# FFN down projection: from seven block products on all 22 contraction tiles to seven on 12 and plain products on 10, with the sums on VectorE

## The chip, the cores and the metric

One core of a Trainium2 chip runs the kernel. The metric is device time in microseconds (us) of one execution; less is better. Besides TensorE (PE in the profile, its weight loads PEld), the core has VectorE (DVE), ScalarE (ACT), GpSimd (POOL) and SyncE (SP), which here issues loads. Each engine works through its own queue in order and waits at semaphores.

## The reference

An encoder block on 512 tokens of width 1024, all in float32: three parallel mixers, a gated merge, an output projection, then the feed-forward network, which the change is about:

```python
def conv_glu_ffn(h, w_up, w_conv, b_conv, w_down):
    a, u = jnp.split(h @ w_up, 2, axis=-1)
    return (jax.nn.gelu(dwconv3(a, w_conv, b_conv)) * u) @ w_down
...
    x = x + conv_glu_ffn(rms_norm(x, ffn_norm_g[l]), w_ffn_up[l], w_ffn_conv[l], b_ffn_conv[l], w_ffn_down[l])
return rms_norm(x, final_norm_g)
```

`h` is 512 x 1024, `w_up` 1024 x 5632, `w_down` 2816 x 1024.

## The kernel before

**Float32 products in three matmuls.** Every operand is split into a high part (ScalarE copies it, rounded, to float32r) and a low part (VectorE subtracts the high part from the source). `mm3` (L192) then issues high x high, high x low, low x high: three matmuls (L193, L194, L195), each 128 x 128 stationary with 512 moving columns.

**Up projection** (loop `for f in range(FT)`, L1331; 22 tiles of 128 hidden columns). For each `f` there are two weight blocks, `ua` and `uu`, of 8 contraction tiles, so 48 matmuls. Each block of 128 x 1024 is loaded (L151) three blocks ahead, and split in two halves (L175 high on ScalarE, L176 low on VectorE) one block ahead, into a ring of four high and four low buffers (`wh`, `wl`). The columns of `ua` then go through a convolution in three steps (L437 to L441) and a gelu (L1355 to L1358); GpSimd multiplies by the norm (L1359), VectorE by the columns of `uu` (L1367). For the first tiles `turn` also transposes the residual on TensorE.

**Down projection.** The 22 contraction tiles are taken as a 2 x 2 block matrix product: rows (two halves of the tokens, `HS` = 256), contraction (two halves of `HF` = 11 tiles), columns (two halves of `S` = 512). Seven block products p1, p5, p6, p3, p7, p2, p4 of sums of blocks replace eight. Each runs over 11 contraction tiles with two token tiles, so 6 matmuls for each weight tile and 462 in all. The sums of weight blocks are made during the up stage: `sum_load` (L1252) loads one contraction tile of all four blocks (1 MB), GpSimd forms four sums (L1261, L1262, L1263, L1258) and stores them to `tdn` in DRAM (L1259). The sums of activations are made by `ops_to` (L1297): the sum on GpSimd (L1309, L1317, L1319), high part on ScalarE (L1322), low part on VectorE (L1324), and p5's further step on VectorE (L1326).

**What sets the order around the change.** A loop over the 77 (product, tile) pairs (L1429) asks for loads four steps ahead (`raws_to`, 1 MB each for four tiles into a unit buffer), for sums two or three steps ahead, and for split tiles four ahead (`tiles_to`, into the same rings of four). Every fourth tile's low part in four of the products is GpSimd's:

```python
A.activation(h, src, AF.Copy)
eng = G if k % 4 == 3 and PRODUCTS[p][0] in ("p1", "p7", "p2", "p4") else V
eng.tensor_tensor(l, src, h.bitcast(F32), op=ALU.subtract)
```

`add` (L1384) adds a finished product to the residual in `xt`: VectorE from PSUM, and for p6 and p7 GpSimd from SBUF (L1395). `unit()` gives one of 15 buffers of 128 x 2112 float32 (`u` in the rows); a load into a unit waits until the last reader of its former content is done. In p4 the last four tiles are done token tile by token tile, the last of them in two column halves, so that the final norm (`squares` L1399, `power` on GpSimd, scale, store) of the earlier rows runs beside them. The framework orders the instructions of each engine when the program is built, so a queue's order isn't the order of the code.

Of the kernel before, what the change touches and what calls it, by code (L numbers as in the profile page):

```python
# [11 lines left out]
F32 = mybir.dt.float32  # L12
# [5 lines left out]
P = 128  # L18
S = 512
# [6 lines left out]
HF = FT // 2  # L26
# [35 lines left out]
def block_list():  # L62
# [19 lines left out]
    for hh in range(2):  # L82
        for f in range(HF * hh, HF * (hh + 1)):
            L.append((("ua", f), 1024))
            L.append((("uu", f), 1024))
# [17 lines left out]
def hybrid_block(ctx, tc, xg, xT, memT, wflat, wdn, vecs, gbias, nabias, out):  # L103
# [1142 lines left out]
    GROUPS = ((0, 4), (4, 8), (8, HF))  # L1246
    B11, B12, B22, B21 = range(4)
    tdn = dp.tile([4, P, HF * S], F32, name="tdn")
# [3 lines left out]
    def sum_load(k):  # L1252
        w = unit()[:, :4 * S]
        SY.dma_start(w.rearrange("p (q n) -> p q n", q=4), wdn[:, :, k * S:(k + 1) * S].rearrange("q p n -> p q n"))
        q = [w[:, i * S:(i + 1) * S] for i in range(4)]

        def store():
            G.tensor_tensor(q[B21], q[B21], q[B22], op=ALU.subtract)  # L1258
            G.dma_start(tdn[:, :, k * S:(k + 1) * S].rearrange("q p n -> p q n"), w.rearrange("p (q n) -> p q n", q=4))  # L1259

        sums.extend([lambda: G.tensor_tensor(q[B11], q[B12], q[B11], op=ALU.subtract),  # L1261
                     lambda: G.tensor_tensor(q[B12], q[B22], q[B12], op=ALU.subtract),  # L1262
                     lambda: G.tensor_tensor(q[B22], q[B22], q[B11], op=ALU.subtract),  # L1263
                     store])


    PRODUCTS = (("p1", wdn, B11), ("p5", tdn, T1), ("p6", tdn, T2), ("p3", wdn, B22), ("p7", tdn, T3), ("p2", wdn, B21),
                ("p4", tdn, T4))
    STEPS = [(p, g) for p in range(7) for g in range(3)]
    TILES = [(p, k) for p in range(7) for k in range(HF)]  # L1270
    uu_ = [[None] * 3 for _ in range(2)]
# [3 lines left out]
    def raws_to(n):  # L1275
        while ahead["raw"] < min(n, len(STEPS)):
            p, g = STEPS[ahead["raw"]]
            a, b = GROUPS[g]
            w = unit()[:, :(b - a) * S]
            SY.dma_start(w, PRODUCTS[p][1][PRODUCTS[p][2], :, a * S:b * S])  # L1280
            for k in range(a, b):
                wraw[p, k] = w[:, (k - a) * S:(k - a + 1) * S]
            ahead["raw"] += 1

    def tiles_to(n):
        while ahead["tile"] < min(n, len(TILES)):
            p, k = TILES[ahead["tile"]]
            src = wraw.pop((p, k))
            h = wp.tile([P, HWT], F32R, tag="hi", name=nm("wh"), bufs=4)[:, :S]
            l = wp.tile([P, HWT], F32R, tag="lo", name=nm("wl"), bufs=4)[:, :S]  # L1290
            A.activation(h, src, AF.Copy)  # L1291
            eng = G if k % 4 == 3 and PRODUCTS[p][0] in ("p1", "p7", "p2", "p4") else V
            eng.tensor_tensor(l, src, h.bitcast(F32), op=ALU.subtract)  # L1293
            wsp[p, k] = h, l
            ahead["tile"] += 1

    def ops_to(n):  # L1297
        while ahead["op"] < min(n, len(STEPS)):
            p, g = STEPS[ahead["op"]]
            name = PRODUCTS[p][0]  # L1300
            nk = GROUPS[g][1] - GROUPS[g][0]
            v = [uu_[i][g][:, :nk * S].rearrange("p (k s) -> p k s", k=nk) for i in range(2)]
            a11, a21, a12, a22 = v[0][:, :, :HS], v[0][:, :, HS:], v[1][:, :, :HS], v[1][:, :, HS:]
            u = unit(F32R)
            h, l = u[:, :nk * HS], u[:, 4 * HS:(4 + nk) * HS]
            r3 = lambda t: t.rearrange("p (k s) -> p k s", s=HS)
            srcs = [(0, nk, {"p1": a11, "p6": a11, "p7": a21, "p2": a12, "p4": a22}.get(name))]
            if name == "p6":
                G.tensor_tensor(a11, a22, a21, op=ALU.subtract)  # L1309
            elif srcs[0][2] is None:  # L1310
                srcs = []
                for k in range(0, nk, 2):
                    m = min(2, nk - k)
# [13 lines left out]
            ops[p, g] = h, l  # L1327
            ahead["op"] += 1

    UR = []  # L1330
    for f in range(FT):  # L1331
        i, j = divmod(f, HF)
        if j % 4 == 0:
            uu_[i][j // 4] = unit()
        UR.append(uu_[i][j // 4][:, j % 4 * S:(j % 4 + 1) * S])
# [23 lines left out]
        G.tensor_tensor(c, c, rb2, op=ALU.mult)  # L1359
        for _ in range(3):  # L1360
            if sums:
                sums.pop(0)()
# [7 lines left out]
        if 2 <= f < FT and f * 3 // 4 - 1 < HF and (f * 3 // 4) != ((f - 1) * 3 // 4):  # L1370
            sum_load(f * 3 // 4 - 1)
# [5 lines left out]
    gfin = wp.tile([P, BW], F32, tag="raw", name=nm("wr"), bufs=3)[:, :D]  # L1377
# [6 lines left out]
    def add(name):  # L1384
        for t in range(2):
# [6 lines left out]
            for c in {"p1": ((0, 0),), "p5": ((0, 1), (1, 1)), "p3": ((0, 1),), "p2": ((0, 0),)}.get(name, ()):  # L1392
# [9 lines left out]
    def power(n):  # L1402
        v, col = tiny(1), tiny(1)
        V.tensor_scalar(v, n[0], n[1], EPS, op0=ALU.add, op1=ALU.add)
        for s in n[2:]:
            V.tensor_tensor(v, v, s, op=ALU.add)
# [3 lines left out]
    def finish(t):  # L1410
        n = []
        squares(t, n, 0, S)
        squares(t, n, S, D)
        col = power(n)
        V.scalar_tensor_tensor(xt[t], xt[t], col, gfin, op0=ALU.mult, op1=ALU.mult)
        SY.dma_start(out[t * P:(t + 1) * P, :], xt[t])

    part = {2: [], 3: []}
    TAIL = HF - 4

    def mms(p, k, t, cs=slice(0, S), ps=None, first=0, end=HF - 1):
        name = PRODUCTS[p][0]
        g, kk = divmod(k, 4)
        h, l = ops[p, g]
        wh, wl = wsp[p, k]
        q = slice(kk * HS + t * P, kk * HS + (t + 1) * P)
        mm3(banks[name][t] if ps is None else ps, h[:, q], l[:, q], wh[:, cs], wl[:, cs], k == first, k == end)

    for j, (p, k) in enumerate(TILES):  # L1429
        name = PRODUCTS[p][0]  # L1430
        last = name == "p4"
        if k == 0:
            pool = atps if name in ("p1", "p5", "p7", "p2") else mmps
            banks[name] = [pool(), pool()]
        if k % 4 == 0:
            i = STEPS.index((p, k // 4))
            raws_to(i + 4)
            ops_to(i + 2 if i == 0 else i + 3)
        tiles_to(j + 4)
        if k == 3 and p > 0:  # L1440
            add(PRODUCTS[p - 1][0])
        if k == 7 and name == "p2":
            for t in (2, 3):
                squares(t, part[t], S, D)
                V.tensor_tensor(xt[t][:, S:], xt[t][:, S:], gfin[:, S:], op=ALU.mult)  # L1445
        if k == 7 and last:
            for t in range(2):
                finish(t)
        if last and k >= TAIL:
            if k == HF - 1:  # L1450
# [134 lines left out]
```

## Time and profile before

| | us |
|---|---|
| timed runs, median of 3 | 884.86 (882.9 to 886.56) |
| the profiled execution's own time | 883.9 |
| its span on the core | 882.0 |
| mean granted TensorE clock | 0.996 |

The page gives for each engine its busy time, share of the span and number of instructions. A row of the timeline gives start, duration, engine, line, operation, output<-inputs, shapes, and in brackets the idle time before it with what ended that. A row of the waits reads: engine, tile and line <- who was waited for: total us, times, longest. In the rows `wr` and `u` are loaded weights, `wh` and `wl` their parts, `mm` and `at` PSUM banks, `s` scratch.

### The profile page before, as it was taken

Reading aid. Unit: us, or ns where it says so; the run is one execution under the profiler, and the core shown is the slowest. Engines: PE = TensorE matmul, PEld = TensorE weight load, DVE = VectorE, ACT = ScalarE, POOL = GpSimd, SP = SyncE. Lnnn points to the kernel's source line nnn. Section 1 sums busy time; section 2 is a strip of 40 time slices with the busy share of each in tenths; the row PEclk is TensorE's granted clock in tenths of the full one; section 3 lists DMA queues with packets and bytes.
Section 4 is the critical chain, followed back from the end, with each engine's and each line's share of the span. In section 5 each row is a group of like instructions: output and inputs, shape, how many; then the busy total and the mean of one; then the engine's idle time right before and its main releaser. Section 6 shows DMA issues by size and latency. Waiting matters only on the chain. (4 is left out here: it accounts for less than half of the span.)

```text
span 882.0 us, 12121 instructions
## 1 busy us (share of the span) xinstructions
PE 858.5 (97%) x4146; PEld 718.5 (81%) x4146; DVE 674.0 (76%) x1306; ACT 486.6 (55%) x1015; POOL 241.6 (27%) x283
## 2 busy tenths in 40 slices
PE   9999999999999999999999999999899999789986
PEld 7898889888888888888888888888787888568865
DVE  7794789996476768897585668778887876989775
ACT  7563476864455668897444453434343444355744
POOL 0101100000435262400000005555665414631142
PEclk9999999999999999999999999999999999999999
DMA  8324633533434363533233425666685533444712
GB/s 271 100 78 153 199 123 101 179 103 96 119 98 105 87 169 120 146 123 111 98 96 122 145 91 205 226 236 234 217 289 177 189 127 133 178 147 153 263 78 96
DMA packets 46014, 131.92 MB, mean 150 GB/s; under 512 B 6008, under 2 KB 11128, under 8 KB 44160
## 3 DMA queue, kind: packets, MB, share of 16 engines
q1 hardware_dynamic: 35168, 112.90, 38.5%
q0 software_dynamic: 10352, 17.85, 6.7%
q8 instruction: 33, 0.54, 0.3%
q10 hardware_dynamic: 432, 0.39, 0.1%
q14 instruction: 29, 0.24, 0.1%
HBM read 115.38 MB, written 15.75 MB: 149 GB/s over the span
## 5 line engine op out<-in xcount | busy, mean ns | idle before, releaser
L195 PE MATMUL mm<-u,wl 128*128 128x512 f32 (+1 forms) x907 | 350.5, 387 | 2.9 <-DVE wl L176 2.9
L193 PE MATMUL mm<-u,wh 128*128 128x512 f32 (+1 forms) x907 | 353.2, 390 | 0.0
L194 PE MATMUL mm<-u,wh 128*128 128x512 f32 (+1 forms) x907 | 349.7, 386 | 0.0
L175 ACT ACTIVATE wh<-wr 128x512 fp32r<-128x512 f32 (+1 forms) x256 | 157.9, 625 | 149.9 <-PE mm L194 117.3
L176 DVE TENSOR_TENSOR wl<-wr,wh 128x512 fp32r<-128x512 f32 (+2 forms) x258 | 196.7, 765 | 47.4 <-ACT wh L175 46.2
L195 PEld LDWEIGHTS mm<-u,wl 128*128 128x128 f32 x907 | 170.3, 188 | 38.9 <-DVE wl L176 4.5
L194 PEld LDWEIGHTS mm<-u,wh 128*128 128x128 f32 x907 | 170.6, 188 | 32.9
L193 PEld LDWEIGHTS mm<-u,wh 128*128 128x128 f32 x907 | 170.6, 188 | 32.6
L1359 POOL TENSOR_TENSOR s<-s,rb 128x512 f32<-128x512 f32 x22 | 36.3, 1648 | 250.3 <-PE mm L195 163.5
L519 POOL DMA_DIRECT2D u<-nav_d x128 | 62.3, 520 | 70.1 <-DVE X L200 25.1
L1293 DVE TENSOR_TENSOR wl<-u,wh 128x512 fp32r<-128x512 f32 x69 | 58.6, 881 | 7.5 <-ACT wh L1291 7.3
L194 PE MATMUL at<-wl,u 128*128 128x512 f32 (+2 forms) x152 | 54.5, 359 | 10.1 <-DVE wl L1293 5.7
L1291 ACT ACTIVATE wh<-u 128x512 fp32r<-128x512 f32 x77 | 46.8, 625 | 30.5 <-PE at L195 12.9
L193 PE MATMUL at<-wh,u 128*128 128x512 f32 (+2 forms) x152 | 53.2, 350 | 2.5 <-ACT wh L1291 2.5
L439 ACT ACTIVATE s<-pad,vec 128x512 f32<-128x512 f32 x30 | 24.4, 813 | 52.9 <-DVE pad L437 52.9
L195 PE MATMUL at<-wh,u 128*128 128x512 f32 (+2 forms) x152 | 52.9, 348 | 0.0
L194 PE MATMUL mm<-wl,u 128*128 128x512 f32 (+1 forms) x118 | 45.2, 383 | 0.4 <-DVE wl L1293 0.4
L195 PE MATMUL mm<-wh,u 128*128 128x512 f32 (+1 forms) x118 | 45.1, 382 | 0.0
L193 PE MATMUL mm<-wh,u 128*128 128x512 f32 (+1 forms) x118 | 44.9, 382 | 0.0
L194 PEld LDWEIGHTS at<-wl,u 128*128 128x128 f32 x152 | 28.9, 190 | 18.2 <-DVE wl L1293 10.4
L1367 DVE SCALAR_TENSOR_TENSOR u<-mm,s 128x512 f32<-128x512 f32 x22 | 15.2, 691 | 26.7 <-POOL s L1359 26.7
L193 PEld LDWEIGHTS at<-wh,u 128*128 128x128 f32 x152 | 28.8, 190 | 7.0 <-ACT wh L1291 3.3
(338 smaller groups left out, 1233.5 us busy)
## 6 DMA issues: line engine op xcount, KB each, us to landing
wr<-wflat SPq DMA_DIRECT2D x125, 512.0 KB, 3.4
u<-wdn SPq DMA_DIRECT2D x17, 1024.0 KB, 6.7
tdn<-u POOLq DMA_DIRECT2D x11, 1024.0 KB, 5.0
u<-tdn SPq DMA_DIRECT2D x8, 1024.0 KB, 5.3
nab<-nabias SPq DMA_DIRECT2D x16, 256.0 KB, 2.7
u<-nav_d POOLq DMA_DIRECT2D x128, 32.0 KB, 2.8
s<-xT SPq DMA_DIRECT2D x15, 256.0 KB, 3.8
u<-tdn SPq DMA_DIRECT2D x4, 768.0 KB, 4.4
```

The source lines that it names most:

```text
L175: A.activation(h[:, u:v], src, AF.Copy)
L176: V.tensor_tensor(l[:, u:v], src, h[:, u:v].bitcast(F32), op=ALU.subtract)
L193: PE.matmul(ps, lh, rh, start=start, stop=False)
L194: PE.matmul(ps, lh, rl, start=False, stop=False)
L195: st["mm"] = PE.matmul(ps, ll, rh, start=False, stop=stop).ins
L439: A.activation(t1, pad[:, 0:512], AF.Identity, scale=vcol(w, i), bias=vcol(b, i))
L519: G.dma_start(vw[r * 32:(r + 1) * 32, i * 256:(i + 1) * 256], nav_v[hf, r, CW[b]:CW[b] + 32, hp * 256:(hp + 1) * 256])
L1291: A.activation(h, src, AF.Copy)
L1293: eng.tensor_tensor(l, src, h.bitcast(F32), op=ALU.subtract)
L1359: G.tensor_tensor(c, c, rb2, op=ALU.mult)
L1367: V.scalar_tensor_tensor(UR[f], pu, 0.5, c, op0=ALU.mult, op1=ALU.mult)
```

## The change

1. The block product now covers only the first 12 contraction tiles (`WN` = 6 in each half). The other 10 (`SN`) are multiplied plainly: column half 1 as segment c1, all 10 tiles behind p3; column half 0 as segments c0, one or two tiles at a time between the products, and its last four at the end. Products and plain segments add up in the same PSUM banks where they can (c1 on p3's; p2 and p4 on c0's).
2. All elementwise sums of this part move from GpSimd to VectorE: the norm factor in the up loop, the sums of weight blocks (now 6 loads for 11), those of activations, the low parts and the adds of products. GpSimd keeps the six stores to `tdn` and the powers of the norm.
3. For f of 12 and more the up loop writes the high and low part of its result itself (`split_act`), since these tiles are used as they are.
4. Weights of the down stage come two tiles (512 KB) at a time for four (1 MB), into the `raw` ring of three buffers for every second load and into a unit otherwise.
5. In the final norm of the last row the second half's sum carries the first half's along (a column of 257), so the sum of the two needs no instruction behind it.

```diff
-HF = FT // 2
+WN = 6
+SN = FT - 2 * WN
+SEGMENTS = (("p1", None), ("c0", (0,)), ("p5", None), ("c0", (1,)), ("p6", None), ("c0", (2,)), ("p3", None),
+            ("c1", range(SN)), ("c0", (3, 4)), ("p7", None), ("p2", None), ("c0", (5,)), ("p4", None),
+            ("c0", range(6, SN)))
...
         def store():
-            G.tensor_tensor(q[B21], q[B21], q[B22], op=ALU.subtract)
+            V.tensor_tensor(q[B21], q[B21], q[B22], op=ALU.subtract)
...
-        sums.extend([lambda: G.tensor_tensor(q[B11], q[B12], q[B11], op=ALU.subtract),
+        sums.extend([lambda: V.tensor_tensor(q[B11], q[B12], q[B11], op=ALU.subtract),
...
     def raws_to(n):
-        while ahead["raw"] < min(n, len(STEPS)):
-            p, g = STEPS[ahead["raw"]]
-            a, b = GROUPS[g]
-            w = unit()[:, :(b - a) * S]
+        while ahead["raw"] < min(n, len(LOADS)):
+            i = ahead["raw"]
+            name, ks, _ = LOADS[i]
+            w = wp.tile([P, BW], F32, tag="raw", name=nm("wr"), bufs=3) if i < 3 or i % 2 else unit()
+            w = w[:, :len(ks) * S]
+            src, q = PRODUCTS[name] if name in PRODUCTS else (wst, int(name[1]))
+            SY.dma_start(w, src[q, :, ks[0] * S:(ks[-1] + 1) * S])
...
             A.activation(h, src, AF.Copy)
-            eng = G if k % 4 == 3 and PRODUCTS[p][0] in ("p1", "p7", "p2", "p4") else V
-            eng.tensor_tensor(l, src, h.bitcast(F32), op=ALU.subtract)
+            V.tensor_tensor(l, src, h.bitcast(F32), op=ALU.subtract)
...
             if name == "p6":
-                G.tensor_tensor(a11, a22, a21, op=ALU.subtract)
+                V.tensor_tensor(a11, a22, a21, op=ALU.subtract)
...
-                        G.tensor_tensor(t, a21[:, sl], a22[:, sl], op=ALU.add)
+                        V.tensor_tensor(t, a21[:, sl], a22[:, sl], op=ALU.add)
                     else:
-                        G.tensor_tensor(t, a12[:, sl], a11[:, sl], op=ALU.subtract)
+                        V.tensor_tensor(t, a12[:, sl], a11[:, sl], op=ALU.subtract)
...
-        G.tensor_tensor(c, c, rb2, op=ALU.mult)
-        for _ in range(3):
-            if sums:
-                sums.pop(0)()
+        V.tensor_tensor(c, c, rb2, op=ALU.mult)
...
-        V.scalar_tensor_tensor(UR[f], pu, 0.5, c, op0=ALU.mult, op1=ALU.mult)
+        if f < 2 * WN:
+            V.scalar_tensor_tensor(ur, pu, 0.5, c, op0=ALU.mult, op1=ALU.mult)
+        else:
+            V.tensor_tensor(c, pu, c, op=ALU.mult)
...
+            split_act(UH[-1], UL[-1], c, 0.5)
...
             for c in {"p6": ((0, 1),), "p7": ((1, 1), (1, 0))}.get(name, ()):
-                G.tensor_tensor(cell(c, t), cell(c, t), Q[t], op=ALU.add)
+                V.tensor_tensor(cell(c, t), cell(c, t), Q[t], op=ALU.add)
...
+    def plain(name, k, t, ps, cs, start, stop):
+        wh, wl = wsp[name, k]
+        tsl = slice(t * P, (t + 1) * P)
+        mm3(ps, UH[k][:, tsl], UL[k][:, tsl], wh[:, cs], wl[:, cs], start, stop)
```

Three places of the engines' queues. Line numbers of the changed kernel are a little higher: L176 is L179 there, L1293 is L1303, L1359 is L1370, L1324 is L1332, L1280 is L1292; a number behind a name is that of the buffer's use.

**VectorE in the up stage, at tile f = 4.** Before, from the convolution's first step (`pad`) to the product with `uu` (L1367):

```order
L437 TENSOR_TENSOR pad0_137<-mm_1120_5922,rb_2_5625 128x512
L176 TENSOR_TENSOR wl_1127_5969<-wr_1106_5867,wh_1126_5968 128x512
L440 SCALAR_TENSOR_TENSOR s_1121_5948<-pad0_137,vec_78,s_1121_5948 128x512
L441 SCALAR_TENSOR_TENSOR s_1121_5948<-pad0_137,vec_78,s_1121_5948 128x512
L176 TENSOR_TENSOR wl_1133_6009<-wr_1115_5912,wh_1132_6008 128x512
L1356 SCALAR_TENSOR_TENSOR s_1122_5952<-s_1122_5952,s_1121_5948 128x512
L1358 SCALAR_TENSOR_TENSOR s_1121_5948<-s_1122_5952,s_1121_5948 128x512
L176 TENSOR_TENSOR wl_1135_6013<-wr_1115_5912,wh_1134_6012 128x512
L1367 SCALAR_TENSOR_TENSOR u_1114_5911<-mm_1128_5972,s_1121_5948 128x512
```

Now, from its second step (L443) on:

```order
L443 SCALAR_TENSOR_TENSOR s_1121_5945<-pad0_137,vec_78,s_1121_5945 128x512
L1264 TENSOR_TENSOR u_1114_5907<-u_1114_5907 128x512
L444 SCALAR_TENSOR_TENSOR s_1121_5945<-pad0_137,vec_78,s_1121_5945 128x512
L179 TENSOR_TENSOR wl_1133_6005<-wr_1115_5909,wh_1132_6004 128x512
L1265 TENSOR_TENSOR u_1114_5907<-u_1114_5907 128x512
L1367 SCALAR_TENSOR_TENSOR s_1122_5949<-s_1122_5949,s_1121_5945 128x512
L1266 TENSOR_TENSOR u_1114_5907<-u_1114_5907 128x512
L179 TENSOR_TENSOR wl_1135_6009<-wr_1115_5909,wh_1134_6008 128x512
L1369 SCALAR_TENSOR_TENSOR s_1121_5945<-s_1122_5949,s_1121_5945 128x512
L1261 TENSOR_TENSOR u_1114_5907<-u_1114_5907 128x512
L1370 TENSOR_TENSOR s_1121_5945<-s_1121_5945,rb_2_5625 128x512
```

The four sums of the weight blocks in `u_1114` and the norm factor (L1370) have moved in between the steps of the gelu and the low parts of the next blocks.

**From the up to the down stage.** Before, GpSimd's queue at the end of the up stage: sums of p5 (L1317) and p6 (L1309), the norm factor of the last up tile (L1359), and the low parts of p1's fourth and eighth tile (L1293):

```order
L1309 TENSOR_TENSOR u_1048_5547<-u_1225_6560,u_1048_5547 128x4x256
L1359 TENSOR_TENSOR s_1379_7455<-s_1379_7455,rb_2_5625 128x512
L1293 TENSOR_TENSOR wl_1395_7515<-u_1372_7417,wh_1394_7514 128x512
L1317 TENSOR_TENSOR s_1430_7658<-u_1178_6285,u_1344_7254 128x256
L1309 TENSOR_TENSOR u_1114_5911<-u_1285_6910,u_1114_5911 128x4x256
L1293 TENSOR_TENSOR wl_1408_7570<-u_1373_7419,wh_1407_7569 128x512
```

Now VectorE's queue at the same place, from the norm factor on (`mm_1383` is the last `uu`):

```order
L1370 TENSOR_TENSOR s_1377_7441<-s_1377_7441,rb_2_5625 128x512
L1303 TENSOR_TENSOR wl_1395_7505<-wr_1371_7405,wh_1394_7504 128x512
L1378 TENSOR_TENSOR s_1377_7441<-mm_1383_7459,s_1377_7441 128x512
L1303 TENSOR_TENSOR wl_1399_7517<-wr_1389_7493,wh_1398_7516 128x512
L1303 TENSOR_TENSOR wl_1402_7529<-wr_1389_7493,wh_1401_7528 128x512
L203 SCALAR_TENSOR_TENSOR u_1356_7320<-s_1377_7441,u_1356_7320 128x512
L1332 TENSOR_TENSOR u_1403_7538<-s_1404_7539,u_1403_7538 128x512
L1332 TENSOR_TENSOR u_1403_7538<-s_1405_7541,u_1403_7538 128x256
L1334 TENSOR_TENSOR u_1048_5547<-u_1048_5547 128x3x256
L1325 TENSOR_TENSOR s_1407_7549<-u_1098_5818,u_1195_6376 128x512
L1325 TENSOR_TENSOR s_1408_7551<-u_1098_5818,u_1195_6376 128x256
L1303 TENSOR_TENSOR wl_1410_7559<-wr_1390_7495,wh_1409_7558 128x512
```

The low parts of p1's tiles 4 to 6 and of c0's first tile (`wl_1410`) share one queue with the sums and low parts of p5's activations; GpSimd has nothing there.

**The weight loads of p5 and p6 in SyncE's queue.** Before, four tiles (three at a product's end) in each:

```order
L1280 DMA u_1390_7505<-tdn_5546 128x2048 [waits DMASW5_49,DMASW2_49,PE_49]
L1280 DMA u_1402_7554<-tdn_5546 128x2048 [waits DMASW7_49,DMASW1_49,PE_49]
L1280 DMA u_1415_7609<-tdn_5546 128x1536 [waits DMAHW4_49,DMASW2_49,DMAHW7_49,DVE_49,Pool_49]
L1280 DMA u_1427_7653<-tdn_5546 128x2048 [waits DMAHW5_49,PE_49]
L1280 DMA u_1441_7711<-tdn_5546 128x2048 [waits DMAHW6_49,DMAHW2_49,DVE_49]
```

Now, with two tiles of p5 (`u_1400`, `wr_1411`, `u_1416`) or p6 (`u_1427`, `wr_1435`, `u_1440`) or p3 (`wr_1461`), or one of c0 (`wr_1419`, `wr_1443`), in each:

```order
L1292 DMA u_1400_7526<-tdn_5546 128x1024 [waits PE_49]
L1292 DMA wr_1411_7568<-tdn_5546 128x1024 [waits DMASW5_49,DMAHW2_49,DMASW4_49,DVE_49]
L1292 DMA wr_1419_7608<-wst 128x512 [waits DMAHW3_49,DVE_49]
L1292 DMA wr_1435_7668<-tdn_5546 128x1024 [waits DMAHW4_49,DVE_49]
L1292 DMA u_1416_7590<-tdn_5546 128x1024 [waits DMASW7_49,DMASW6_49,DMAHW6_49,DVE_49,Activation_49]
L1292 DMA wr_1443_7708<-wst 128x512 [waits DMAHW7_49,DVE_49]
L1292 DMA u_1427_7636<-tdn_5546 128x1024 [waits DMAHW2_49,DVE_49]
L1292 DMA wr_1461_7776<-wdn 128x1024 [waits DMAHW5_49,DMAHW0_49,DVE_49]
L1292 DMA u_1440_7690<-tdn_5546 128x1024 [waits DMAHW4_49,DVE_49]
```

`u_1400`, `u_1416`, `u_1427` and `u_1440` are one and the same buffer in the built program, and so are the two units that follow for p3 (`u_1453`, `u_1466`): each of these loads waits for VectorE's low part of the second tile of the one before it.

More of the change, by code (lines that the diff above doesn't have):

```diff
@@ L102, in hybrid_block @@
 @with_exitstack
-def hybrid_block(ctx, tc, xg, xT, memT, wflat, wdn, vecs, gbias, nabias, out):
+def hybrid_block(ctx, tc, xg, xT, memT, wflat, wdn, wst, vecs, gbias, nabias, out):
     nc = tc.nc
@@ L1407, in power @@
+    last = NT - 1
+    V.tensor_tensor(xt[last][:, :S], A4[last], xt[last][:, :S], op=ALU.add)
+    ends = [atps(), atps()]
+    tk = list(SEGMENTS[-1][1])
+    def power(v):
+        col = tiny(1)
         G.tensor_tensor(col, v, nhalf[:, :1], op=ALU.pow)
         return col
[L1410 to L1450, printed above, removed]
-                V.tensor_tensor(cell((1, 0), 1), banks["p4"][1], cell((1, 0), 1), op=ALU.add)
-                for kk in range(TAIL, HF):
-                    mms(p, kk, 0)
-                ends = [mmps(), mmps()]
-                for e in range(2):
-                    for kk in range(TAIL, HF):
-                        mms(p, kk, 1, slice(e * HS, (e + 1) * HS), ends[e][:, :HS], TAIL)
-            continue
-        mms(p, k, 0)
-        mms(p, k, 1, end=TAIL - 1 if last else HF - 1)
@@ L1462, in hybrid_block, with mean @@
[L1462 to L1473 removed]
+    def mean(n):
+        v = tiny(1)
+        V.tensor_scalar(v, n[0], n[1], EPS, op0=ALU.add, op1=ALU.add)
+        return v
```

188 lines of the change are left out of this document (128 added, 60 removed).

## The prediction

> **What bounds the kernel now.** I read four views in this order: the page's busy times, the busy time by stage, the waits of TensorE, and the timeline around its longest waits. Numbers are microseconds (us) unless marked.
>
> ```profile
> PE 858.5 (97%) x4146; PEld 718.5 (81%) x4146; DVE 674.0 (76%) x1306; ACT 486.6 (55%) x1015; POOL 241.6 (27%) x283
> ```
> ```profile
> 527.00:751.30 224.30, 221.41 (x990) 182.29 (x989) 176.31 (x205) 90.90 (x151) 117.45 (x81) 1.00 0.58 202
> 751.30:875.00 123.70, 110.81 (x475) 87.29 (x473) 103.44 (x124) 69.59 (x121) 43.62 (x28) 0.99 0.42 151
> ```
> The stages are the up projection (from 527) and the down projection (751.3 to 875). In each row stand the length, then the busy time of PE, PEld, DVE, ACT and POOL. TensorE is busy 97% of the span, so only two things can move the time: the number of matmuls, and the stalls between them. Nearly all that is lost lies in the down stage.
>
> ```profile
> 751.26 0.39 PE L193 MATMUL at<-wh,u 128*128 128x512 f32 x1
> 755.34 0.39 PE L193 MATMUL at<-wh,u 128*128 128x512 f32 x1
> 759.91 0.79 PE L194 MATMUL at<-wl,u 128*128 128x512 f32 x1 [4.19 <-POOL wl L1293]
> ...
> 872.00 0.28 PE L193 MATMUL mm<-wh,u 128*128 128x256 f32 x1
> ...
> 874.75 0.28 PE L195 MATMUL mm<-wh,u 128*128 128x256 f32 x1
> ```
> The first two rows are the first and the nineteenth matmul of the down stage: 4.08 for 18 gives a pitch of **0.2267**. The last two are the first and the last of 24 half-width ones: 2.75 for 23 gives 0.1196. The stage holds 7 products x 11 tiles x 6 = 462 matmuls, of which 12 are issued as those 24 halves: 450 x 0.2267 + 24 x 0.1196 = 104.9. It lasts from 751.26 to 874.75 + 0.12, 123.6. So **18.7 are stalls**. The view of waits names them:
>
> ```profile
> PE at L194 <- DVE wl L1293: 5.7, 7, 1.5
> PE at L194 <- POOL wl L1293: 4.2, 1, 4.2
> PE at L193 <- ACT wh L1291: 2.5, 2, 2.2
> ```
> The rest of the 18.7 is what a stall costs before and after the wait that is shown. Each of these waits is for the high or low part of a weight tile. Why they are late shows beside the longest one:
>
> ```profile
> 753.67 2.76 POOL L1309 TENSOR_TENSOR u<-u,u 128x1024 f32<-128x1024 f32 x1 [3.16 <-DVE u L1326]
> 756.39 2.24 POOL L1359 TENSOR_TENSOR s<-s,rb 128x512 f32<-128x512 f32 x1
> 758.60 1.26 POOL L1293 TENSOR_TENSOR wl<-u,wh 128x512 fp32r<-128x512 f32 x1
> ```
> ```profile
> 752.38 1.22 DVE L1326 TENSOR_TENSOR u<-u 128x1024 f32<-128x1024 f32 x1
> ...
> 754.11 3.40 DVE L1326 TENSOR_TENSOR u<-u 128x1024 f32<-128x1024 f32 x1
> ```
> The low part that TensorE wants is third in GpSimd's queue. And VectorE's row at 754.11 takes 3.40 where the same form took 1.22 at 752.38: beside GpSimd's sums it stands still. The up stage has the same fault:
>
> ```profile
> 623.03 4.93 DVE L176 TENSOR_TENSOR wl<-wr,wh 128x512 fp32r<-128x512 f32 x1
> ```
> ```profile
> 623.67 1.29 POOL L1261 TENSOR_TENSOR u<-u 128x512 f32<-128x512 f32 x1
> 624.92 1.28 POOL L1359 TENSOR_TENSOR s<-s,rb 128x512 f32<-128x512 f32 x1
> 626.15 1.25 POOL L1262 TENSOR_TENSOR u<-u 128x512 f32<-128x512 f32 x1
> ```
> ```profile
> 625.27 0.39 PE L194 MATMUL mm<-u,wh 128*128 128x512 f32 x1
> 628.02 0.50 PE L195 MATMUL mm<-u,wl 128*128 128x512 f32 x1 [2.36 <-DVE wl L176]
> 628.36 0.40 PE L193 MATMUL mm<-u,wh 128*128 128x512 f32 x1
> ```
> ```profile
> PE mm L195 <- DVE wl L176: 2.9, 3, 2.4
> ```
> One low part was held for 4.93 by three GpSimd sums. The stall cost 2.75 - 0.23 = 2.52, and the slow restart to 628.36 another 0.11, where the view says 2.36. There are three such waits, 2.9 together; at some 0.25 more for each, the up stage loses about **3.6**.
>
> **The change, part by part.** The sum is made against the profiled execution: span 882.0, own time 883.9; the three timed runs have a median of 884.9, so I add 1.0 at the end.
>
> *More matmuls.* Seven products on 6 tile pairs are 7 x 6 x 6 = 252, ten plain tiles are 10 x 4 token tiles x 2 column halves x 3 = 240: 492 for 462, with 24 half-width ones at the end as before. 30 x 0.2267 = **+6.8**, and nothing hides it.
>
> *GpSimd's work goes to VectorE.* What VectorE takes for it while GpSimd is quiet:
>
> ```profile
> 683.58 0.68 DVE L176 TENSOR_TENSOR wl<-wr,wh 128x512 fp32r<-128x512 f32 x1
> 684.18 0.69 DVE L437 TENSOR_TENSOR pad<-mm,rb 128x512 f32<-128x512 f32 x1
> ```
> ```profile
> 822.59 0.96 DVE L1324 TENSOR_TENSOR u<-u,u 128x768 fp32r<-128x768 f32 x1
> 823.47 0.69 DVE L1293 TENSOR_TENSOR wl<-u,wh 128x512 fp32r<-128x512 f32 x1
> ```
> ```profile
> L1359 POOL TENSOR_TENSOR s<-s,rb 128x512 f32<-128x512 f32 x22 | 36.3, 1648 | 250.3 <-PE mm L195 163.5 <-DVE s L1358 86.8
> ```
> From start to start VectorE needs 0.60 for 512 columns and 0.88 for 768 (256 columns: 0.32, estimated on the same line); GpSimd 1.6. In the up stage VectorE has ten such instructions in each of the 22 up tiles; the change adds L1370 to each, four sums to six of them, and a low part to the last ten. The fullest tile holds 15, about 9.5 with the longer conv steps, beside 48 matmuls x 0.2267 = 10.9. So VectorE keeps up, the 81 GpSimd items of the stage row shrink to six stores, and the three stalls go: **-3.6**. The cover is the two up blocks by which low parts run ahead; were it gone, each us that VectorE is late would be one of TensorE. A sum also waits for its 1 MB load, now on VectorE:
>
> ```profile
> u<-wdn SPq DMA_DIRECT2D x17, 1024.0 KB, 6.7
> ```
> The second group of sums stands eight rows of VectorE's queue behind the low part that lets its load go, 5 to 8 with what these rows wait for, and two loads go out together there; so I expect 0 to 2 of waiting, under the same cover.
>
> *Stalls of the down stage.* By the waits above, they go with GpSimd's queue: **-18.7**, if nothing takes their place. What takes their place is my main unknown.
>
> *New waits.* Weights now come two tiles (512 KB) at a time. Every second load goes to the only unit buffer left for them: u_1416 needs the low part of u_1400's second tile, u_1427 that of u_1416, and so on for five loads, until the c1 tiles free more. One round is load, high part, low part:
>
> ```profile
> wr<-wflat SPq DMA_DIRECT2D x8, 512.0 KB, 3.3
> u<-tdn SPq DMA_DIRECT2D x8, 1024.0 KB, 5.3
> ```
> ```profile
> L1291 ACT ACTIVATE wh<-u 128x512 fp32r<-128x512 f32 x77 | 46.8, 625 | 30.5 <-PE at L195 12.9
> ```
> A load of 512 KB from tdn is not in the trace. Bounds: 3.3, the same size from wflat, and 5.3, double the size from tdn; I take 3.3, the row of its size. Let T be the end of the last up matmul. From T - 0.4 VectorE has 21 instructions up to the low part of p5's second tile: 14 x 0.60 + 3 x 0.88 + 4 x 0.32 = 12.3, done at T + 12. The load issued then lands at T + 15.4 and its high part is ready at T + 16.1. VectorE, by then at the sums of p6 and the adds of p1 (seven instructions, 5.0), reaches its low part at T + 17.0 and ends it at T + 17.7. TensorE wants it after p1 (8.2), one plain tile (2.7), four tiles of p5 (5.4) and three matmuls that need only the high part (0.7): T + 17.0 to 17.1. So p5's fifth tile waits **0.6**. Walked on in the same way, p6's first tile waits 0.6 (its load issued at T + 18.5), p3's first 0.5 (behind the adds of p6), and three others 0.1. That is 2.0, with six slow restarts at 0.1 it is 2.6; with some more for loads in flight two at a time I take **+3.5**. Bounds: 0 (a wait can't be negative), and +10 if each of the five loads takes 5.3, since then every round is 2.0 longer and no buffer absorbs it.
>
> [...]
>
> *The rest of the down stage.* Loads after c1 have more buffers, and twelve plain tiles of 2.7 give VectorE slack. The adds of p7 (L1414) cost VectorE 4 x 0.60 inside p2's 8.2; by the same walk no low part is late there.
>
> *The end.*
>
> ```profile
> 876.50 0.16 DVE L1470 TENSOR_TENSOR y<-y,y 128x1 f32<-128x1 f32 x1 [0.45 <-ACT s L1399]
> 876.74 0.55 POOL L1471 TENSOR_TENSOR y<-y,nhalf 128x1 f32<-128x1 f32 x1 [1.93 <-DVE y L1470]
> ```
> The last sum of squares now goes straight to the power: L1470's step falls out of the chain, 876.74 - 876.50 = **-0.2**.
>
> Sum: 883.9 + 6.8 - 3.6 - 18.7 + 3.5 - 0.2 = 871.7; on the scale of the timed runs **872.7**.
>
> **The rivals.** (1) *The loads are never late*: the waits of p5, p6 and p3 are hidden, as the c0 tiles between them give 2.7 each. 872.7 - 3.5 = 869.2. For it: in the walk each is late by under 1. Against: VectorE's queue up to T + 18 has no gap.
>
> (2) *One buffer sets the pace.* If the loads take about 5.3 each, five rounds cost +10 for +3.5: 879.2, and with some of the up stage's gain lost 880 to 882, no measurable change. [...] Against: only about 0.42 of the DMA engines' time is used in this stage.
>
> (3) *The old stalls are not all GpSimd's.* Only the wait named POOL goes (759.91 - 755.34 - 0.23 = 4.3) and those in the up stage, and the other 14.4 stay, since a high part may only be written when the tile four before it is done. 872.7 + 14.4 - 3.5 = 883.6, no change. Against it:
>
> ```profile
> L1293 DVE TENSOR_TENSOR wl<-u,wh x69: 674/684/2886, 743.8 to 870.6; 128x512 fp32r<-128x512 f32 x69
> ```
> The shortest, the median and the longest of VectorE's low parts, in ns: a form that takes 684 and once 2886 is held by something, and GpSimd is what it was held by above.
>
> (4) *Slower*: the same single buffer, at the worst landing that a 512 KB load from wflat had in the up stage:
>
> ```profile
> DMA to landing us min/median/max: 3.1/3.6/7.4
> ```
> At 7.4 each of the five rounds is 4.1 over my value: 872.7 + 20.5 - 3.5 = 889.7. It is slower than before from a landing of 6.4 on. For it: loads from tdn and wst now run beside each other. Against: the median is 3.6, and the worst came with 1 MB loads and stores around it, which this stage no longer has.
>
> **How the numbers follow.** Forecast 872.7 (870.5 to 877): 0.52. Rival 1: 0.20. Rivals 2 and 3, from 878 to 884: 0.20. Rival 4: 0.06. Further gains that I don't see: 0.02. A measurement of this kernel can tell about 0.5% (4.4) from no change, so faster means below 880.4: the first two, a third of the third group and the last, 0.81; the same 0.12; slower 0.07 (rival 4 and a little of 2). The range runs from just below rival 1 to the start of the no-change cases: 868 to 880.
>
> **What would show it.** Right: GpSimd empty from 527 on but for six stores and the five powers; no PE wait on L179's low parts in the up stage; VectorE's low parts at 0.7 throughout; 492 matmuls in a down stage of about 115 (111.7 of matmuls and 3 to 4 of waits), the waits on the low parts of p5, p6 and p3. Wrong: loads from tdn into the unit buffer that land after 4.5 or more; stretched VectorE rows without GpSimd beside them; waits in p7, p2 or p4.

## The result and the profile after

The changed kernel takes **872.41 us** (median of 4, 872.38 to 872.85), the kernel before, run beside it, 884.56 (median of 4, 882.9 to 886.56): ratio 0.9863, interval 0.9842 to 0.9884. 872.7 was predicted. The span is 870.6 at a granted clock of 0.998.

Busy times of the changed kernel, from its page:

```profile
PE 861.0 (99%) x4176; PEld 723.3 (83%) x4176; DVE 644.0 (74%) x1365; ACT 481.7 (55%) x1003; POOL 87.2 (10%) x184
```

The same by stage (up, down; columns as before), and the groups of GpSimd from 527 on:

```profile
527.00:747.00 220.00, 220.00 (x987) 182.24 (x986) 169.57 (x260) 100.61 (x160) 4.59 (x6) 1.00 0.46 154
747.00:863.00 116.00, 114.85 (x506) 92.18 (x504) 79.43 (x126) 54.51 (x98) 1.54 (x3) 1.00 0.42 135
```
```profile
L1262 POOL DMA_DIRECT2D tdn<-u x6 | 4.6, 765 | 230.8 <-DVE u L1261 230.8
L1486 POOL TENSOR_TENSOR y<-y,nhalf 128x1 f32<-128x1 f32 x5 | 2.7, 545 | 262.5 <-DVE y L1491 261.6 <-ACT s L1512 0.9
```

TensorE has no gap left in the up stage, and GpSimd only six stores and five powers. VectorE does more instructions (1365 for 1306) in less busy time (644.0 for 674.0): what it had lost was standing, not work. Its low parts show it, shortest, median and longest in ns; the longest was 2886 before:

```profile
L1303 DVE TENSOR_TENSOR wl<-wr,wh x31: 681/689/696, 742.4 to 850.0; 128x512 fp32r<-128x512 f32 x31
L1303 DVE TENSOR_TENSOR wl<-u,wh x30: 684/691/694, 758.0 to 852.7; 128x512 fp32r<-128x512 f32 x30
```

The first and the last matmul of the down stage, and the waits of TensorE (PE) and its weight loads (PEld) from 527 on:

```profile
747.08 0.39 PE L196 MATMUL at<-wh,u 128*128 128x512 f32 x1
...
862.72 0.28 PE L198 MATMUL at<-wh,u 128*128 128x256 f32 x1
```
```profile
PEld at L197 <- DVE wl L1303: 2.4, 5, 0.8
...
PEld at L196 <- ACT wh L1302: 2.1, 4, 0.6
...
PE at L197 <- DVE wl L1303: 0.3, 1, 0.3
PE mm L196 <- ACT wh L1302: 0.3, 1, 0.3
PE at L196 <- ACT wh L1302: 0.2, 1, 0.2
```

The down stage starts 4.2 earlier (747.08 for 751.26) and lasts 115.8, of which 480 x 0.2267 + 24 x 0.1196 = 111.7 are matmuls: 4.1 of stalls for 18.7. From the end of the last matmul to the end of the span it takes 7.8 for 7.1. So -4.2 + 6.8 - 14.6 + 0.6 = -11.4, the difference of the spans. The view of waits counts only 0.8 of the 4.1 at the matmuls. At the weight loads, whose time overlaps that of the matmuls (723.3 beside 861.0 in a span of 870.6), it counts 5.6 (0.7 and 0.4 in rows not shown), and all of it is for high and low parts of weight tiles. Neither sum is the stall, which is read from the starts of the matmuls.

### The profile page after: what moved, and what is told of

The parts are those of the page before. It is cut to its first block, busy times and chain, and to the rows that moved or that the text cites. A ratio compares the mean times of both kernels' runs of the same rounds, so it can differ in the third digit from the quotient of the medians.

```text
span 870.6 us, 12096 instructions
## 1 busy us (share of the span) xinstructions
PE 861.0 (99%) x4176; PEld 723.3 (83%) x4176; DVE 644.0 (74%) x1365; ACT 481.7 (55%) x1003; POOL 87.2 (10%) x184
## 4 chain that ended last, share of the span: by engine, by line
PE 97%; DVE 1%; ACT 1%; issue 0%; DMA 0%; POOL 0%; POOLq 0%; ACTq 0%
PE mm L196 26%; PE mm L198 26%; PE mm L197 26%; PE at L197 4%; PE at L198 4%; PE at L196 4%; PE at L964 1%; PE at L945 1%; PE at L926 0%; PE at L927 0%; PE at L747 0%; PE at L795 0%; PE at L1052 0%; PE at L1244 0%; DVE u L1518 0%
## 5 line engine op out<-in xcount | busy, mean ns | idle before, releaser
L179 DVE TENSOR_TENSOR wl<-wr,wh 128x512 fp32r<-128x512 f32 (+2 forms) x258 | 175.5, 683 | 53.8 <-ACT wh L178 51.9
L197 PE MATMUL at<-wl,u 128*128 128x512 f32 (+2 forms) x172 | 60.0, 349 | 0.4 <-DVE wl L1303 0.3
L198 PE MATMUL at<-wh,u 128*128 128x512 f32 (+2 forms) x172 | 59.4, 346 | 0.0
L196 PE MATMUL at<-wh,u 128*128 128x512 f32 (+2 forms) x172 | 58.9, 348 | 0.4 <-ACT wh L1302 0.2
L197 PE MATMUL mm<-wl,u 128*128 128x512 f32 x108 | 42.2, 391 | 0.0
L198 PE MATMUL mm<-wh,u 128*128 128x512 f32 x108 | 42.1, 390 | 0.0
L196 PE MATMUL mm<-wh,u 128*128 128x512 f32 x108 | 41.6, 391 | 0.3 <-ACT wh L1302 0.3
L197 PEld LDWEIGHTS at<-wl,u 128*128 128x128 f32 x172 | 32.4, 188 | 6.2 <-DVE wl L1303 2.4
L196 PEld LDWEIGHTS at<-wh,u 128*128 128x128 f32 x172 | 32.1, 188 | 5.8 <-ACT wh L1302 2.1
L198 PEld LDWEIGHTS at<-wh,u 128*128 128x128 f32 x172 | 32.4, 189 | 3.8
L1303 DVE TENSOR_TENSOR wl<-u,wh 128x512 fp32r<-128x512 f32 x30 | 20.1, 690 | 14.1 <-ACT wh L1302 14.0
L1302 ACT ACTIVATE wh<-u 128x512 fp32r<-128x512 f32 x30 | 18.2, 626 | 20.9 <-PE at L198 9.5
L1302 ACT ACTIVATE wh<-wr 128x512 fp32r<-128x512 f32 x32 | 19.6, 624 | 18.4 <-PE at L198 7.7
```

The costliest lines, as they stand in the source:

```text
L179: V.tensor_tensor(l[:, u:v], src, h[:, u:v].bitcast(F32), op=ALU.subtract)
L196: PE.matmul(ps, lh, rh, start=start, stop=False)
L197: PE.matmul(ps, lh, rl, start=False, stop=False)
L198: st["mm"] = PE.matmul(ps, ll, rh, start=False, stop=stop).ins
L1303: V.tensor_tensor(l, src, h.bitcast(F32), op=ALU.subtract)
```

## The experiments

Eleven kernels, five rounds each beside the kernel before, whose medians there were 884.3 to 884.7. The table has their medians, and from the profile of each the start of the down stage, its matmuls (462, 480 or 492, priced as above), its stalls, and the end behind the last matmul. The last four columns are those of the one execution that was profiled; some kernels differ more from one execution to the next (before 881.9 to 887.6, e9 878.7 to 881.8) than others (e1 862.5 to 863.1).

| kernel | median | down starts | matmuls | stalls | end |
|---|---|---|---|---|---|
| before | 884.56 | 751.26 | 104.9 | 18.7 | 7.1 |
| changed | 872.41 | 747.08 | 111.7 | 4.1 | 7.8 |
| e1: before, all on VectorE | 862.71 | 747.21 | 104.9 | 1.6 | 7.2 |
| e2: changed, back on GpSimd | 878.74 | 747.91 | 111.7 | 8.6 | 7.8 |
| e10: before, up stage on VectorE | 877.13 | 747.12 | 104.9 | 15.6 | 7.2 |
| e8: before, down sums on VectorE | 873.14 | 751.17 | 104.9 | 8.1 | 7.1 |
| e9: before, low parts on VectorE | 881.04 | 751.40 | 104.9 | 15.4 | 7.1 |
| e3: changed, one unit more | 869.25 | 747.81 | 111.7 | 0.5 | 7.7 |
| e11: changed, loads in two halves | 868.87 | 747.28 | 111.7 | 0.4 | 7.8 |
| e4: changed, sums two ahead | 868.32 | 747.05 | 111.7 | 0.0 | 7.7 |
| e5: e4, tail sum apart | 868.36 | 747.79 | 111.7 | 0.0 | 7.5 |
| e6: e4, products on 16 tiles | 866.54 | 747.43 | 109.0 | 0.1 | 8.1 |
| e7: e1, sums two ahead | **861.51** | 747.08 | 104.9 | 0.5 | 7.2 |

**The two halves of the change apart.** e1 moves GpSimd's elementwise work to VectorE in the kernel before and leaves the products on all 22 tiles:

```diff
-            G.tensor_tensor(q[B21], q[B21], q[B22], op=ALU.subtract)
+            V.tensor_tensor(q[B21], q[B21], q[B22], op=ALU.subtract)
...
-            eng = G if k % 4 == 3 and PRODUCTS[p][0] in ("p1", "p7", "p2", "p4") else V
-            eng.tensor_tensor(l, src, h.bitcast(F32), op=ALU.subtract)
+            V.tensor_tensor(l, src, h.bitcast(F32), op=ALU.subtract)
...
-        G.tensor_tensor(c, c, rb2, op=ALU.mult)
+        V.tensor_tensor(c, c, rb2, op=ALU.mult)
```

> The kernel before with all its GpSimd sums, every fourth low part and the adds of p6 and p7 moved to VectorE; the seven products stay on all 22 contraction tiles (462 matmuls in the down stage). Theory (the old stalls come from GpSimd's queue, the split of the tiles only costs its 30 matmuls): the up stage loses its three stalls (-3.6 to -4.2), most of the 18.7 of the down stage goes, and as VectorE has about 92 of work in 105 of matmuls there, 5 to 10 of new waits come: 866 to 872, so level with the changed kernel or a little better. Rival (the smaller number of product tiles carries the gain): 878 to 885, as the sums are as many as before and now stand in front of the low parts.

e2 puts the moved work back on GpSimd in the changed kernel, with one low part in each of p1, p7, p2 and p4 for two:

```diff
-        V.tensor_tensor(c, c, rb2, op=ALU.mult)
+        G.tensor_tensor(c, c, rb2, op=ALU.mult)
...
-                        V.tensor_tensor(t, a21[:, sl], a22[:, sl], op=ALU.add)
+                        G.tensor_tensor(t, a21[:, sl], a22[:, sl], op=ALU.add)
```

> The changed kernel with the moved work put back on GpSimd: norm factor, sums of weight blocks, sums of activations, the low part of tile 3 in p1, p7, p2 and p4, adds of p6 and p7; the split into 12 and 10 tiles stays. Theory: three or so up stalls come back (+3 to +4), and of the old down stalls about what the smaller number of sums leaves, 18 product tile sums for 33, so +6 to +12: 881 to 888, no better than before. Rival (the split carries the gain): 872 to 876.

Its edit also moves four subtractions of 128x256 in an earlier stage (L680, 0.74 each for 0.42), which the change had left on VectorE. They cost about 0.3: a row behind them (L681) starts at 178.4 for 178.1.

e1 came to 862.71 (ratio to before 0.9747, 0.9731 to 0.9763), better than expected and **9.7 better than the changed kernel**; e2 to 878.74 (0.9934, 0.9919 to 0.9949), between both theories. So the move of engine alone is worth 22, the split (with the smaller loads and the new end that come with it) 6, and together they give 12. The up stage's stalls hardly came back in e2: one gap of 0.57 for 0.23 is left, where three or so were expected. With GpSimd in use the split helps, 8.6 of stalls for 18.7, presumably since there are fewer sums; no run changes their number alone. Once GpSimd is out of it, the split only costs: 6.8 of matmuls, 2.5 more stalls (4.1 for 1.6) and 0.6 at the end, less 0.1 by an earlier start: 9.8, where the medians differ by 9.7. e7 and e4, further down, are the same pair with nearly all stalls gone, and differ by 6.8, the 30 matmuls. My fear for e1, that VectorE would be too full, was wrong. The down stage of e1:

```profile
747.20:853.80 106.60, 106.17 (x475) 87.01 (x473) 98.77 (x151) 69.75 (x120) 2.03 (x3) 1.00 0.50 176
```

VectorE is busy 98.8 of 106.6, and TensorE loses only 1.6: here a queue that was 93% full did little harm, and nothing in it seems to have been held, as its low parts took 0.68 to 0.70. What can hold it shows in e2, where VectorE and GpSimd work on these tiles side by side (rows of both at the start of the down stage):

```profile
754.55 0.94 DVE L1335 TENSOR_TENSOR u<-u 128x768 f32<-128x768 f32 x1
755.58 2.22 POOL L1318 TENSOR_TENSOR u<-u,u 128x768 f32<-128x768 f32 x1 [1.49 <-DVE u L1335]
756.02 2.32 DVE L1304 TENSOR_TENSOR wl<-wr,wh 128x512 fp32r<-128x512 f32 x1
757.75 1.74 POOL L1328 TENSOR_TENSOR s<-u,u 128x512 f32<-128x512 f32 x1
758.27 2.11 DVE L1333 TENSOR_TENSOR u<-s,u 128x512 fp32r<-128x512 f32 x2
```

The low part at 756.02 takes 2.32 instead of 0.69: it ends at 758.34, 0.54 behind GpSimd's row (757.80), about its own length.

**The move of engine in three parts.** All three start from the kernel before. e10 moves only the up stage's work (norm factor, sums of weight blocks), e8 only the down stage's sums and the adds, e9 only the low parts. e9's edit:

```diff
-            eng = G if k % 4 == 3 and PRODUCTS[p][0] in ("p1", "p7", "p2", "p4") else V
-            eng.tensor_tensor(l, src, h.bitcast(F32), op=ALU.subtract)
+            V.tensor_tensor(l, src, h.bitcast(F32), op=ALU.subtract)
```

e8's:

```diff
-                G.tensor_tensor(a11, a22, a21, op=ALU.subtract)
+                V.tensor_tensor(a11, a22, a21, op=ALU.subtract)
...
-                G.tensor_tensor(cell(c, t), cell(c, t), Q[t], op=ALU.add)
+                V.tensor_tensor(cell(c, t), cell(c, t), Q[t], op=ALU.add)
```

and e10's:

```diff
-        G.tensor_tensor(c, c, rb2, op=ALU.mult)
+        V.tensor_tensor(c, c, rb2, op=ALU.mult)
...
-            G.tensor_tensor(q[B21], q[B21], q[B22], op=ALU.subtract)
+            V.tensor_tensor(q[B21], q[B21], q[B22], op=ALU.subtract)
```

> The kernel before with only the down stage's sums of activations and the adds of p6 and p7 on VectorE; the up stage's sums and every fourth low part in four products stay on GpSimd. Theory (low parts are late because GpSimd's sums stand in front of them and hold VectorE's rows beside them): most of the 18.7 goes, 866 to 870. Rival (it is the low parts on GpSimd themselves that are late): 878 or above.

> The kernel before with only the eight late low parts (every fourth tile of p1, p7, p2, p4) on VectorE; all sums stay on GpSimd. Theory (sums and low parts on GpSimd each hold part of the 18.7, and e8 left 8.1 of it): 4 to 9 less than before, 876 to 881. Rival (the wait named POOL alone goes, 4.3, and low parts behind held VectorE rows stay late): 880 to 882.

> The kernel before with only the up stage's GpSimd work (norm factor and sums of weight blocks) on VectorE. Theory (it removes the three up stalls and nothing else): the first matmul of the down stage at 747.1 to 747.4 for 751.26, and 3.6 to 4.2 less, 880.3 to 881. Rival (the sums were also what delayed GpSimd at the start of the down stage): 875 to 879.

Of the 18.7 of stalls e8 takes 10.6, e9 3.3 and e10 3.1, and e10 the 4.1 of the up stage besides; their sum in the down stage, 17.0, is the 17.1 of e1. The columns of one execution each are too rough to say that the parts add up to a tenth. e8 took less than expected. e9 missed: its 3.3 is less than the 4 to 9 expected, and its time lies in the rival's range, but not by the rival's mechanism, since the wait that was named POOL did not go (below). For e10 the rival was right: GpSimd's work from the up stage also reaches into the down stage, as the norm factor at 756.39, ahead of the low part in the prediction's rows, suggests.

e9 shows best that the engine named in a wait need not be the cause. The wait at p1's fourth tile that was GpSimd's (4.19) is now put down to VectorE, and is longer:

```profile
754.25 3.42 DVE L1325 TENSOR_TENSOR u<-u 128x1024 f32<-128x1024 f32 x1
758.82 0.69 DVE L1366 SCALAR_TENSOR_TENSOR u<-mm,s 128x512 f32<-128x512 f32 x1 [1.15 <-POOL s L1358]
...
760.57 3.99 DVE L1292 TENSOR_TENSOR wl<-u,wh 128x512 fp32r<-128x512 f32 x2
```
```profile
753.81 2.78 POOL L1308 TENSOR_TENSOR u<-u,u 128x1024 f32<-128x1024 f32 x1 [3.15 <-DVE u L1325]
756.53 2.26 POOL L1358 TENSOR_TENSOR s<-s,rb 128x512 f32<-128x512 f32 x1
759.66 1.57 POOL L1316 TENSOR_TENSOR s<-u,u 128x256 f32<-128x256 f32 x1 [0.87 <-DVE u L1366]
761.19 2.82 POOL L1308 TENSOR_TENSOR u<-u,u 128x1024 f32<-128x1024 f32 x1
```
```profile
761.83 0.80 PE L194 MATMUL at<-wl,u 128*128 128x512 f32 x1 [5.74 <-DVE wl L1292]
```

The low part that TensorE wants now stands in VectorE's queue, and that queue is late by GpSimd twice: the row at 754.25 takes 3.42 for 1.22 beside GpSimd's sum, and the last product of the up stage (758.82) waits for GpSimd's norm factor. The low parts themselves then run beside two more rows of GpSimd, two of them in 3.99.

And e8 shows the same the other way round. GpSimd's only work there is a low part, 1.30 as a rule; this one takes 5.95, while VectorE works without a break:

```profile
836.09 5.95 POOL L1293 TENSOR_TENSOR wl<-u,wh 128x512 fp32r<-128x512 f32 x1 [4.35 <-issue]
```
```profile
836.42 0.68 DVE L1445 TENSOR_TENSOR u<-u,wr 128x512 f32<-128x512 f32 x1
837.03 1.21 DVE L1324 TENSOR_TENSOR u<-u,u 128x1024 fp32r<-128x1024 f32 x1
...
839.63 1.28 DVE L1293 TENSOR_TENSOR wl<-u,wh 128x512 fp32r<-128x512 f32 x2
```

It ends at 842.04, 1.13 behind VectorE's last row (840.91), so nearly its usual 1.30 lies behind VectorE's work. Six instructions of VectorE start while it runs. My reading of both rows, e2's 2.32 for 0.69 and this 5.95 for 1.30, is that one of the two engines was held while the other worked; by what, no run shows. What share of the 22 is this holding, and what share GpSimd's own longer time (1.30 for 0.69 for the same low part), no run separates.

**The new waits.** e3 loads the final norm's factor later (the change had put it into a unit; before, it lay in the `raw` ring), so that one unit more is free while p1 to p3 run; e4 asks for sums two groups ahead for three; e11 gives the unit loads of p5, p6 and p3 two halves of one unit in turn.

```diff
-    gfin = unit()[:, :D]
-    SY.dma_start(gfin, gbias[16:].partition_broadcast(P))
...
+        if name == "c1":
+            gfin = unit()[:, :D]
+            SY.dma_start(gfin, gbias[16:].partition_broadcast(P))
```
```diff
-                ops_to(OPS.index((name, k // GN)) + (2 if j == 0 else 3))
+                ops_to(OPS.index((name, k // GN)) + 2)
```
```diff
+            if i >= 3 and i % 2 == 0 and i <= HALVES:
+                if not pair:
+                    pair.append(unit())
+                w = pair[0][:, i // 2 % 2 * 1024:(i // 2 % 2 + 1) * 1024]
```

> The changed kernel with the final norm's factor loaded after c1 and not at the end of the up stage, so that its unit buffer serves loads and sums while p1 to p3 run. Theory (the new waits at p5, p6 and p3, together about 4.1, come from too few units: one for the loads, two for the sums): all but the wait at c0's first tile (0.8) go, 2 to 3.3 less than the changed kernel, 869 to 870.5. Rival (VectorE's queue is simply full there): no change, 872 to 873.

> The changed kernel with sums of activations asked for two groups ahead and not three, so that their high parts, which wait for a unit that TensorE still reads, no longer stand in front of the weight tiles' parts on ScalarE and VectorE. Theory (the waits at the fifth tile of p5, p6 and p3 are those of low parts behind such sums): 1 to 2.5 less than the changed kernel, 870 to 871.5. Rival (landing of the loads in their one unit sets these waits): no change; if the sums then come too late, 1 to 3 more.

> The changed kernel with the unit loads of p5, p6 and p3 going in turn to the two halves of one unit, so that none waits for the parts of the load just before it; sums stay three groups ahead. Theory A (the prediction's: the single buffer of the loads sets the waits at p5, p6 and p3): about 3 of the 4.1 go, 869 to 870. Theory B (after e4: ScalarE stands 2.4 to 3.6 at the high part of a sum whose unit TensorE still reads, with the high parts of weight tiles behind it): the loads land earlier and it helps little, 871.3 to 872.5.

All three take the waits away (869.25, 868.32, 868.87 for 872.41), e4 all of them and more than it was expected to. (c0's first tile, put at 0.8 in e3's expectation, lost 0.3 in the changed kernel: the row there stands for four matmuls.) After e4 I held a second theory: in the changed kernel ScalarE waits mostly at the high part of a sum whose unit TensorE still reads (five waits):

```profile
ACT u L1330 <- PE at L198: 15.3, 5, 3.6
```

e11 keeps the sums where they are and mends only the loads; the same wait there (the line is six lower down):

```profile
ACT u L1336 <- PE at L198: 2.1, 3, 0.7
```

So theory B fell: that wait was a consequence, TensorE being late by the load. The single buffer was the cause, as predicted. Its loads in the changed kernel, by SyncE's rows:

```profile
759.34 0.32 SPq L1292 DMA_DIRECT2D u<-tdn  x1
...
765.75 0.32 SPq L1292 DMA_DIRECT2D u<-tdn  x1
...
771.70 0.32 SPq L1292 DMA_DIRECT2D u<-tdn  x1
...
778.03 0.33 SPq L1292 DMA_DIRECT2D u<-wdn  x1
...
783.69 0.33 SPq L1292 DMA_DIRECT2D u<-wdn  x1
```
```profile
u<-tdn SPq DMA_DIRECT2D x4, 512.0 KB, 3.8
```

Four rounds take 24.35, 6.1 each, of which 3.8 is the landing; in a round TensorE has four tiles or two and a plain one, 24 x 0.2267 = 5.4. That is 0.65 too long on average. By the starts of the matmuls, the tiles that the five loads bring (p5's fifth, p6's first and fifth, p3's first and fifth) lose 0.95, 0.5, 0.8, 0.2 and 1.0, 3.5 of the 4.1. In e4 the units come free in another order, and the load that was issued at 759.34 starts at 755.82.

**How much split.** e6 puts the products on 16 tiles, with e4's edit:

```diff
-WN = 6
+WN = 8
...
-            ("c1", range(SN)), ("c0", (3, 4)), ("p7", None), ("p2", None), ("c0", (5,)), ("p4", None),
-            ("c0", range(6, SN)))
+            ("c1", range(SN)), ("p7", None), ("p2", None), ("p4", None),
+            ("c0", range(2, SN)))
```

> The changed kernel with sums two groups ahead (868.3), and the seven products on 16 tiles, 6 plain: 7 x 8 x 6 + 6 x 24 = 480 matmuls for 492, and three units for plain activations for five. Theory (the split costs its matmuls and nothing else, VectorE needs no plain tiles as slack): 12 x 0.2267 = 2.7 less, 865.3 to 866. Rival (plain tiles are the cover of VectorE's sums): waits of 2 or more at p5 to p3 take it back, 868 or above.

866.54: 1.8 less, not 2.7. The matmuls fell by 2.7 and no stall came; 0.35 went to a longer end and 0.4 to a later start of the stage, of which 0.3 was there in the profiled execution from its first 38 us on. With the sums two groups ahead, the plain tiles aren't needed as cover. e7 is the other extreme, e1 with its sums two groups ahead:

```diff
-            ops_to(i + 2 if i == 0 else i + 3)
+            ops_to(i + 2)
```

> The kernel before with all sums on VectorE (862.7) and sums of activations two groups ahead for three. Theory (its last waits, 1.6 in the down stage, are low parts behind such sums): 861 to 861.8. Rival (with 7 products on 22 tiles a sum asked for later is late itself): 863 to 866.

861.51 (0.974, 0.9726 to 0.9754), the best of all: 23 better than before and 10.9 better than the changed kernel.

**The end.** e5 is e4 with the sum of the last row's halves as an instruction of its own again:

```diff
-                A.activation(scr(HS + e), z[:, e * HS:(e + 1) * HS + e], AF.Square, scale=D ** -0.5, accum_out=v)
+                A.activation(scr(HS), z[:, cs], AF.Square, scale=D ** -0.5, accum_out=v)
...
+            V.tensor_tensor(y, v0, v, op=ALU.add)
```

> The changed kernel with sums two groups ahead (868.3) and, besides, the last row's two half sums of squares added by an instruction of their own again, as in the kernel before. Theory (the carried column lengthens the end: the last square waits for a product that waits for a power on GpSimd, 7.9 from the last matmul to the end of the span for 7.25 before): 0.4 to 0.6 less, 867.7 to 867.9. Rival (the end is longer for another reason, such as the scale of the row before): no change, 868.2 to 868.5.

The times don't tell them apart (868.36 for 868.32). In the profile the end is 0.24 shorter, but that execution runs 0.7 late from its first 38 us on (so does e3's), which hides it there; how the other executions start isn't on record. What makes the end longer is to be read from the changed kernel's rows of VectorE:

```profile
863.14 0.75 DVE L1518 SCALAR_TENSOR_TENSOR u<-u,y,u 128x512 f32<-128x512 f32 x1 [0.65 <-POOL y L1486]
863.81 0.21 DVE L1491 TENSOR_SCALAR y<-y,y 128x1 f32<-128x1 f32 x1
863.94 0.42 DVE L1510 TENSOR_TENSOR u<-at,u 128x256 f32<-128x256 f32 x1
864.67 0.16 DVE L1515 SCALAR_TENSOR_TENSOR u<-y,y 128x1 f32<-128x1 f32 x1 [0.32 <-POOL y L1486]
```
```profile
864.92 0.42 ACT L1512 ACTIVATE s<-u 128x257 f32<-128x257 f32 x1 [1.06 <-DVE u L1515]
```

The last matmul ends at 862.84, yet its sum (L1510) starts at 863.94, behind the scale of the row before (L1518), which waited for a power; and the last square waits for L1515, which waits for a power as well. In the kernel before that sum started 0.64 behind the last matmul (875.51 for 874.87), also behind the scale of the row before; now it is 1.10. This 0.46 stands in e4 and e5 alike, and no run undoes it.

## Why the prediction was right, by its steps

- *More matmuls, +6.8*: right. 4176 matmuls for 4146, and the down stage of e4, with no stall, lasts the 111.7 of its matmuls.
- *Up stage, -3.6*: right. The start of the down stage moved by 4.2, of which 0.3 was there at 38 us already, a difference of the two executions. e10, which moves this stage's work alone, moves that start by 4.1. No sum's wait for its load reached TensorE.
- *Stalls of the down stage, -18.7*: right. e1 removes them without the split, all but 1.6. But the prediction showed two causes, GpSimd's queue and rows of VectorE that stand still beside it, and then priced only the queue's going. e9 shows that the queue is only a part: a low part moved out of it is late on VectorE as well.
- *New waits, +3.5*: right in cause (e11) and nearly in size, 4.1. The walk had the loads of p5's fifth and p6's first tile go out at T + 12 and T + 18.5; with T at 747.08, 759.34 and 765.75 are T + 12.3 and T + 18.7. It was right for p5's fifth tile to within 0.4 (0.95 for 0.6, from 763.61 to 765.47 less the matmuls between), for p6's first (0.5 for 0.6) and, less so, for p3's first (0.2 for 0.5). The term that was too small is "three others 0.1": p6's fifth tile lost 0.8 and p3's fifth 1.0. The landing was 3.8, not 3.3. The walk with its restarts gave only 2.6; the 0.9 that was added for loads in flight, without a row for it, is what brought the term near, and that is luck in part. Counting rounds (here 6.1, known only afterwards, against 5.4) is the shorter way to such a term.
- *The rest of the stage*: right, no stall after 790.
- *The end, -0.2*: wrong in sign, +0.6. The step counted the instruction that falls out (L1470) and not what the carried column waits for, nor that the last row's sum, which stands behind the scale of the row before in both kernels, is reached 0.46 later.
- *The sum*: the terms missed by -0.6, +0.6 and +0.8, together +0.8; and the 1.0 added for the scale of the timed runs wasn't there, as the changed kernel's median is its span and 1.8 (the profiled execution of before: 1.9). So the 0.3 between 872.7 and 872.41 is errors that cancel.
- *Rivals*: (1) is what e3, e4 and e11 make of the kernel (868.3 to 869.3 for 869.2), so its condition was the buffer, not the plain tiles between. (2) and (4) needed landings of 5.3 and 7.4; the median was 3.8. (3) fell with e1: 17.1 of 18.7 go, where it left 14.4.

What the prediction didn't ask is which half of the change pays. Its own sum held the answer: +6.8 and +3.5 belong to the split, and only the move of engine stands against them.

## What to carry to other kernels

Where VectorE and GpSimd both do elementwise work beside a full TensorE, as here, try pricing them as one engine: an item of GpSimd cost its own length (1.30 for VectorE's 0.69 for a low part) and what it held of VectorE's queue (a row of 1.22 that took 3.40 or 3.42), and VectorE alone at 93% did better here than both together (862.71 for 884.56). When a change has two parts, run each alone: here one was worth -22 and the other +9.7 on top of it. For a single buffer that loads take one after the other, compare its round (landing, parts, release) with the consumer's work in a round (here 6.1 against 5.4), before walking single waits.

## What the runs showed of the hardware

After some of the long stalls TensorE ran at a granted clock of 0.51 to 0.54 for 3.1 to 3.4 us. In e8, behind a gap of 3.04 between two matmuls (length, busy times, and the granted clock, 0.54, before the DMA share):

```profile
842.00:845.50 3.50, 3.41 (x8) 2.69 (x9) 0.30 (x1) 0.63 (x1) 0.04 (x1) 0.54 0.00 0
```

Matmuls follow each other there at 0.43 instead of 0.2267, which costs 8 x 0.2 = 1.6 more than the stall itself. The same stands behind the 4.57 of the kernel before (0.51 from 759.9 to 763.0), but not behind a gap of 3.38 in e10 (1.00 from 757.3 to 761.0), so the length of the gap alone doesn't decide it; what does, no run shows.
